# A streaming encoder trunk on one core: weights moved to multiples of 256 bytes, low parts first, the first norm one half product later, states in a pool of their own

## The chip, the core and the metric

The kernel runs on one core of one Trainium2 chip. The metric is the device time of one execution in microseconds, the median of three executions.

## What is computed

Two layers over 288 frames at once (256 of a new stream, 32 of a running one), width 2048, all in float32. Cut to what matters here:

```python
h = rmsnorm(x, g)                       # layer 0: retention and gated linear attention side by side
z = einsum('btd,de->bte', h, w_in)      # 2048 x 7184
o = concat(retention heads with state_ret, GLA heads with state_gla)   # 4 + 4 heads
x = x + einsum('bte,ed->btd', o, w_out)
g, u = split(rmsnorm(x) @ w_up)         # ConvFFN, D_FF = 5632
x = x + (silu(conv3(g)) * u) @ w_down
x = x + band_attention(rmsnorm(x) @ w_qkv) @ w_out_att    # layer 1: 16 heads
x = x + ConvFFN(rmsnorm(x)); y = rmsnorm(x)
```

Returned are y, the new retention and GLA states, the new keys and values and the last rows of each ConvFFN.

## The kernel before, in words

Features lie on the 128 partitions, the 288 frames (`T`) along the free axis. Every weight matrix is cut into tiles of 128 x 128; one product (128 outputs for all frames) sums over 16 tiles of its input (22 in the down projections), which arrive 8 at a time (`WCH`) as one DMA of 512 KB on SP's queue.

To keep float32 precision with the fast float32r matmul, each operand is split into a high part (rounded to float32r) and a low part (the rest). `weights` (L55) does this for a chunk of 8 weight tiles: `w` comes in, ScalarE casts it to `wh` (L62), VectorE subtracts to get `wl` (L63). The inputs `xx` (16 tiles of 2 x 288 numbers) and `bb` hold both parts of an input side by side, high first: bytes 0 to 1151 high, 1152 to 2303 low. For each weight tile TensorE then does three matmuls into one PSUM accumulator, which I call a triple:

- L91: `wh` times the first 320 columns (`TX`) of the pair, from byte 0: all 288 high ones, 32 low ones;
- L92: `wh` times the other 256 columns, from byte 1280, added to columns 32 to 287;
- L95: `wl` times the 288 high columns, from byte 0.

`joined` (L97) adds the 32 columns that went behind. In the built program every tile of `xx` and `bb` starts at a multiple of 256 bytes of its partition. The tiles `wh` and `wl` (three buffers each, 4096 bytes) start at 64 bytes past a multiple of 256, since the constants ahead of them end there; one weight tile of 128 columns is 512 bytes, so each of them starts 64 past a multiple. The exception is `lo_h`, the weights of the 16 gate columns in `first_products`, at 192 past one.

Tile, the layer the kernel is written in, sets the order on each engine from the order of the code and its own costs; each engine runs its queue in order. `run` (L210) opens the stages one after another, each with a pool of SBUF of its own: `in` (`start`, L262), `ab` (`ab_mixer`, layer 0's heads), then `x` with `f0`, `c` and `f1` in it. A pool's memory is given to the next one.

Around the places that change:

- `start` loads inputs and first weights in 12 pieces (`first_products`, L104), then does one value product `v0`, then the sum of squares on ScalarE and VectorE (`first_squares`, L144 to L155), then `norm_stat` (L202; its matmul is L207, then `rsqrt`, L164 to L174, which gives `R`), then the first half (`second(0)`, 8 triples) of the product `v1`. Its second half is `first[4](1)` in `gla_head` (L562), the first gate's matmul (L513) needs `R`.
- Each GLA head loads its state (`gst`, L567, 128 KB) and each retention head its own (`rst`, L738, 256 KB) into the pool `ab`, by DMA issued from GpSimd (POOL). The retention states are updated in place and written out by L832.
- `out_proj` (L289) for layer 0 loads `x` again by DMA from POOL (L294, 288 KB each). L304 adds a finished product to `x`; ScalarE and VectorE then prepare the next norm (L184 to L200).

Of the kernel before, what the change touches and what calls it, by code (L numbers as in the profile page):

```python
# [5 lines left out]
F32 = mybir.dt.float32  # L6
# [6 lines left out]
P = 128  # L13
D = 2048
KD = D // P
TP = 256
TS = 32
T = TP + TS
# [8 lines left out]
RANK = 16  # L27
# [5 lines left out]
GRP = P // TS  # L33
# [5 lines left out]
class Trunk:  # L39
# [52 lines left out]
        nc.tensor.matmul(ps[:, TX - T : T], lhsT=w, rhs=x[:, TX:], start=False, stop=last, skip_group_check=True)  # L92

    def high(self, ps, w, x, last):
        self.nc.tensor.matmul(ps[:, :T], lhsT=w, rhs=x[:, :T], start=False, stop=last, skip_group_check=True)  # L95

    def joined(self, ps):  # L97
        n = TX - T
# [111 lines left out]
    def run(self, ctx):  # L210
        nc, a = self.nc, self.a

        ones = self.const("ones", [P, P + 32])
        self.ones, self.eps = ones[:, :P], ones[:, P : P + 1]
        self.xx = [self.const(f"x{k}", [P, 2 * T], F32R) for k in range(KD)]
        self.xh, self.xl = [[x[:, c] for x in self.xx] for c in (slice(0, T), slice(T, 2 * T))]
        b_all = self.const("b", [P, KD, 2 * T], F32R)
        self.bh_all, self.bl_all = b_all[:, :, :T], b_all[:, :, T:]
        self.bb, self.bh, self.bl = [[x[:, k, :] for k in range(KD)] for x in (b_all, self.bh_all, self.bl_all)]
        self.R = self.const("R", [P, T])  # L220
        nc.vector.memset(self.ones, 1.0)
        nc.vector.memset(self.eps, EPS)
        self.gains = self.const("gains", [P, 5, KD], F32, a["gains"], nc.scalar)
        self.sq_last = None
        with self.tc.tile_pool(name="in", bufs=1) as pool:
            sums = self.start(pool)
        with self.tc.tile_pool(name="ab", bufs=1) as pool:
            self.ab_mixer(pool, *sums)
        with self.tc.tile_pool(name="x", bufs=1) as xp:

            x = xp.tile([P, KD * T + 16], F32, name="x", tag="x")[:, : KD * T].rearrange("p (k t) -> p k t", t=T)
            self.x = [x[:, k, :] for k in range(KD)]
            self.out_proj(a["w_out_ab"], 1, (WCH, 0), x)
            with self.tc.tile_pool(name="f0", bufs=2) as pool:
                self.ffn(pool, 0, 2, x)
            with self.tc.tile_pool(name="c", bufs=2) as pool:
                self.chain(
                    self.att_heads(pool), 3,
                    lambda: self.out_start(a["w_out_att"], (0, WCH), 2),
                )  # L240
            self.out_proj(a["w_out_att"], 3, (0, WCH))
            with self.tc.tile_pool(name="f1", bufs=2) as pool:
                self.ffn(pool, 1, 4, x)
# [18 lines left out]
    def start(self, pool):  # L262

        nc, a = self.nc, self.a
        w = a["w_in"]

        nc.scalar.activation(self.R[:, :1], self.ones[:, :1], AF.Abs_reciprocal_sqrt)
        xw = self._one(pool, "xw", [P, KD, T + N_FIRST * P + RANK])
        x_in = xw[:, :, :T]
        self.x = [x_in[:, k, :] for k in range(KD)]  # L270


        lo_h = self._one(pool, "lo_h", [P, KD, P], None, F32R)
        nc.gpsimd.memset(lo_h.bitcast(F32)[:, :, 2 * RANK :], 0.0)
        k0, q0, lo_ps = self.first_products(a["x_first"], xw, lo_h)
        self.ident = self.const("ident", [P, P], F32, a["ident"], nc.sync)

        self.w2 = self.const("w2", [P, 512 + 224])[: 2 * RANK + 1, :512]
        nc.sync.dma_start(self.w2, a["w2"])
        v0 = self.input_product(w[VB])  # L280
        self.first_squares(x_in)

        self.norm_stat()
        v1 = self.mm()
        second = lambda part: self.project(w[VB + 1], self.xx, KD, chunks=(0, WCH), part=part, ps=v1)
        second(0)
        return k0, q0, v0, lo_ps, second

    def out_proj(self, w, n, chunks, load=None):  # L289
# [23 lines left out]
    def ffn(self, pool, layer, n, x_all):  # L313
        nc, a = self.nc, self.a
        bb = self.bb + [self._one(pool, f"b{k}", [P, 2 * T], None, F32R) for k in range(KD, HALF)]
# [7 lines left out]
        last = layer == 1  # L323
        for half in range(2):
            for fl in range(HALF):
                f = half * HALF + fl
                g = self.input_product(up[f])
                u = self.input_product(up[NF + f])
                gp = gps[f % 3]
                nc.gpsimd.tensor_copy(gp[:, TP + 2 : TP + 4], hist[:, f, :])  # L330
                nc.vector.tensor_tensor(gp[:, 2 : TP + 2], g[:, :TP], self.R[:, :TP], op=ALU.mult)  # L331
                nc.vector.tensor_tensor(gp[:, TP + 4 :], g[:, TP:], self.R[:, TP:], op=ALU.mult)
                nc.gpsimd.tensor_copy(conv_out[:, f, 0:2], gp[:, TP : TP + 2])  # L333
                nc.gpsimd.tensor_copy(conv_out[:, f, 2:4], gp[:, T + 2 : T + 4])
                cw = convp[:, f, :]
                W = T + 2
                gc = pool.tile([P, W], F32, name="gc", tag="gc")
                nc.vector.tensor_scalar(gc, gp[:, 0:W], cw[:, 0:1], cw[:, 3:4], op0=ALU.mult, op1=ALU.add)
                for w in (1, 2):
                    nc.vector.scalar_tensor_tensor(  # L340
                        gc, gp[:, w : w + W], cw[:, w : w + 1], gc, op0=ALU.mult, op1=ALU.add
                    )
                s = pool.tile([P, W], F32, name="sg", tag="sg")
                nc.scalar.activation(s, gc, AF.Silu)
                v = pool.tile([P, T], F32, name="v", tag="v")
                nc.vector.tensor_tensor(v, u, self.R, op=ALU.mult)  # L346
                nc.vector.tensor_tensor(v[:, :TP], v[:, :TP], s[:, :TP], op=ALU.mult)
                nc.vector.tensor_tensor(v[:, TP:], v[:, TP:], s[:, TP + 2 :], op=ALU.mult)  # L348
                self.split(bb[fl][:, :T], bb[fl][:, T:], v)
            if last and half == 1:  # L350
                nc.scalar.activation(self.R[:, :1], self.ones[:, :1], AF.Abs_reciprocal_sqrt)
            if half == 1:
                nc.gpsimd.dma_start(a["conv_out"][:, layer], conv_out)
            for m in range(KD):
                ps = self.project(down[m], bb, HALF, half * HALF)
                nc.vector.tensor_tensor(self.x[m], self.x[m], ps, op=ALU.add)
                if half == 1:
                    if last:
                        self.square_in(m, m == KD - 1)
                        nc.scalar.activation(self.x[m], self.x[m], AF.Copy, scale=self.gains[:, n, m : m + 1])  # L360
                    else:
                        self.norm_in(m, n)
# [188 lines left out]
    def gla_head(self, pool, hd, w, sums, masks, eyem, hg, s4, sts, first):  # L551
        nc, a = self.nc, self.a
        k = first[0] if first else self.input_product(w[KB + hd])
        k = self.parted(pool, k, "k0", s4["k"][:, 0, hd, :])
# [3 lines left out]
        v = first[2] if first else self.input_product(w[VB + 2 * hd])  # L558
        v = [self.parted(pool, v, "v0", s4["v"][:, 0, hd, :])]
# [3 lines left out]
        v.append(self.parted(pool, v1, "v1", s4["v"][:, 1, hd, :]))  # L563
        gate = lambda i: self.gate(pool, w[GB + 2 * hd + i], i, s4["z"][:, i, hd, :])
        z = [gate(0)] if first else []
        st = pool.tile([P, 256], F32, name="gst", tag="gst", bufs=GRP)
        nc.gpsimd.dma_start(st, a["state_gla"][hd])  # L567
        sts.append(st)

# [14 lines left out]
        vt = self.to_tokens(pool, v, "vt", 256, bufs=2)  # L586
# [6 lines left out]
        for i, l in enumerate(LEVELS):  # L593
            qk = pool.tile([P, TP], F32, name="qk", tag="qk", bufs=3)
            self.decayed(qk, k, q, E[:, i, :], l)
            for t in range(2):
                x = qk[:, t * P : (t + 1) * P]
                rhs = _halves(x, l)[:, :, 1, :]
# [7 lines left out]
        ps = self.mm()[:, : 3 * P]  # L606
        nc.tensor.matmul(ps[:, :P], lhsT=qk[:, :P], rhs=qk[:, P:], start=True, stop=True)
        for t in range(2):
            c = slice(t * P, (t + 1) * P)
# [123 lines left out]
    def ret_head(self, pool, hd, w, cosR, sinR, kdec, hg, s4, sts, aside):  # L733
        nc, a = self.nc, self.a
        dec = pool.tile([P, 384], F32, name="dec", tag="dec")
        nc.gpsimd.dma_start(dec, a["dec"][hd])
        st = pool.tile([P, 2, 256], F32, name="rst", tag="rst", bufs=GRP)
        nc.gpsimd.dma_start(st, a["state_ret"][hd])  # L738
        sts.append(st.rearrange("p j v -> p (j v)"))

        def rope(base, name):
            z = [self.input_product(w[base + 2 * hd + i]) for i in range(2)]
# [9 lines left out]
        k = rope(KA, "k")  # L752
# [167 lines left out]
    def att_sample(self, pool, g, kept, v4, bd):  # L920
# [10 lines left out]
            nc.tensor.matmul(ps[c], lhsT=q[:, TP:], rhs=k[:, TP:], start=True, stop=True)  # L931
        pv = self.mm()[:, :P]
        nc.tensor.transpose(pv, v4[0].rearrange("p h t -> p (h t)"), self.ident)
        vt = pool.tile([P, P], F32, name="avt4", tag="avt4")
        nc.scalar.copy(vt, pv)
        s = pool.tile([P, T], F32, name="as4", tag="as4")
        own = pool.tile([P, GRP, TS], F32, name="own4", tag="own4")
        mx = pool.tile([P, 1], F32, name="mx4", tag="mx4")
        sm = pool.tile([P, 1], F32, name="sm4", tag="sm4")
        nc.vector.tensor_tensor(s, ps, bias, op=ALU.add)  # L940
        nc.vector.tensor_reduce(mx, s, axis=mybir.AxisListType.X, op=ALU.max, negate=True)
        nc.scalar.activation(s, s, AF.Exp, bias=mx, accum_out=sm)
# [18 lines left out]
        for i in range(2):  # L961
            for c, (_, _, vc) in zip(quarter, kept):
                nc.tensor.matmul(
                    po[c], lhsT=pT[:, 1 + i, c], rhs=vc[:, i, :], start=False, stop=i == 1, skip_group_check=True
                )
        o = pool.tile([P, P], F32, name="ao4", tag="ao4")
        nc.vector.tensor_scalar(o, po, sm, None, op0=ALU.mult)
        yield
        ps = self.mm()[:, :P]
# [139 lines left out]
```

## Time and profile before

| | |
|---|---|
| median of 3 runs | 2658.73 us (2657.0 to 2659.18) |
| the profiled execution's own time | 2656.71 us |
| its span, first to last instruction | 2654.9 us |
| mean granted TensorE clock | 0.997 |
| busy: TensorE, VectorE, ScalarE, GpSimd | 99%, 64%, 42%, 9% |
| read from and written to HBM | 434.69 MB and 10.40 MB, 168 GB/s over the span |

Every number below that is a duration or a start comes from this one profiled execution. In rows of the timeline the first column is the start in us from the span's start, the second the duration. Matmuls overlap in their pipeline: what a matmul costs is the step from its start to the next one's, not its duration. In rows of the windows view the columns are the window, its length, the busy time and count of each engine, the granted clock of TensorE, and the DMA engines' share and GB/s.

### The profile page before, as it was taken

To read this page: it belongs to the slowest core of one execution; us is meant where nothing else is said; L and a number is where in the kernel's file an instruction comes from. 1 tells how busy PE (TensorE), PEld (TensorE's weight loads), DVE (VectorE), ACT (ScalarE), POOL (GpSimd) and SP (SyncE) were. 2 spreads that over 40 slices of the span, in tenths; PEclk is the share of its full clock that TensorE was granted. 3 is DMA by queue.
4 is the path that set the end of the run, shared out by engine and by line. 5 is a ranking of instruction groups with operands and counts; after the bars stand their busy time and mean duration, and the time that the engine had idled before them with its cause. 6 is when DMAs were issued, how large, how long until landed. Compare 5 with 4: busy or idle time off the path is not lost.

```text
span 2654.9 us, 49383 instructions
## 1 busy us (share of the span) xinstructions
PE 2636.5 (99%) x20079; PEld 2618.0 (99%) x20079; DVE 1708.6 (64%) x3355; ACT 1123.6 (42%) x1511; POOL 228.9 (9%) x471
## 2 busy tenths in 40 slices
PE   9999999999999999999999999999999999999998
PEld 9999999999999999999999999999999999999997
DVE  8776666677775467776555555567777645777654
ACT  6554444443333333334444344444333333333443
POOL 3000001011110001110021110100111000111000
PEclk9999999999999999999999999999999999999999
DMA  6444555555555555555675565555555555555554
GB/s 231 152 132 160 161 162 168 184 166 167 168 167 162 169 171 168 167 170 163 169 213 181 177 188 167 160 168 165 169 167 170 161 168 173 167 167 168 166 169 132
DMA packets 127584, 448.31 MB, mean 169 GB/s; under 512 B 16155, under 2 KB 16475, under 8 KB 127356
## 3 DMA queue, kind: packets, MB, share of 16 engines
q1 hardware_dynamic: 119564, 424.47, 52.0%
q0 software_dynamic: 7648, 20.65, 2.5%
q8 instruction: 157, 2.57, 0.4%
q14 instruction: 71, 0.58, 0.1%
q10 hardware_dynamic: 144, 0.04, 0.0%
HBM read 434.69 MB, written 10.40 MB: 168 GB/s over the span
## 4 chain that ended last, share of the span: by engine, by line
PE 87%; issue 11%; DMA 0%; DVE 0%; POOL 0%; ACT 0%; DVEq 0%; POOLq 0%; ACTq 0%
PE acc L91 32%; PE acc L95 28%; PE acc L92 25%; PE mm L599 0%; PE mm L913 0%; PE mm L877 0%; DMA x<-in_xT 0%; DMA out_ret_out<-rst 0%; DVE y L370 0%; PE mm L876 0%; PE mm L207 0%; PE mm L914 0%; DMA gains<-in_gains 0%; PE mm L91 0%; PE mm L513 0%
## 5 line engine op out<-in xcount | busy, mean ns | idle before, releaser
L91 PE MATMUL acc<-x,wh 128*128 128x320 f32 x4464 | 1394.9, 313 | 0.3 <-DVE x L185 0.3
L62 ACT CAST wh<-w 128x1024 fp32r<-128x1024 f32 (+1 forms) x812 | 838.8, 1033 | 1288.1 <-PE acc L92 1044.7
L63 DVE TENSOR_TENSOR wl<-w,wh 128x1024 fp32r<-128x1024 f32 (+1 forms) x812 | 977.5, 1204 | 532.8 <-ACT wh L62 521.1
L95 PE MATMUL acc<-x,wl 128*128 128x288 f32 x4464 | 1298.4, 291 | 0.0
L92 PE MATMUL acc<-x,wh 128*128 128x256 f32 x4464 | 1246.5, 279 | 0.0
L91 PEld LDWEIGHTS acc<-x,wh 128*128 128x128 f32 x4464 | 838.4, 188 | 2.3 <-issue 1.1
L92 PEld LDWEIGHTS acc<-x,wh 128*128 128x128 f32 x4464 | 838.5, 188 | 0.8 <-issue 0.3
L95 PEld LDWEIGHTS acc<-x,wl 128*128 128x128 f32 x4464 | 836.9, 188 | 0.1
L91 PE MATMUL acc<-b,wh 128*128 128x320 f32 x1920 | 599.0, 312 | 1.9 <-ACT wh L62 1.9
L95 PE MATMUL acc<-b,wl 128*128 128x288 f32 x1920 | 560.3, 292 | 0.5 <-DVE wl L63 0.5
L92 PE MATMUL acc<-b,wh 128*128 128x256 f32 x1920 | 536.6, 280 | 0.0
L91 PEld LDWEIGHTS acc<-b,wh 128*128 128x128 f32 x1920 | 361.6, 188 | 2.7 <-ACT wh L62 2.4
L95 PEld LDWEIGHTS acc<-b,wl 128*128 128x128 f32 x1920 | 361.4, 188 | 1.1 <-DVE wl L63 0.8
L92 PEld LDWEIGHTS acc<-b,wh 128*128 128x128 f32 x1920 | 361.6, 188 | 0.0
L100 DVE COPY tail<-acc 128x32 f32<-128x32 f32 x376 | 72.0, 192 | 285.7 <-PE acc L95 282.9
L333 POOL COPY conv_out<-gp 128x2 f32<-128x2 f32 x88 | 100.3, 1140 | 1272.5 <-DVE gp L331 1272.5
L161 ACT CAST b<-v 128x288 fp32r<-128x288 f32 x88 | 38.1, 433 | 149.8 <-DVE v L348 149.8
L340 DVE SCALAR_TENSOR_TENSOR gc<-gp,convp,gc 128x290 f32<-128x290 f32 x176 | 91.8, 522 | 6.2
L101 DVE TENSOR_TENSOR acc<-acc,tail 128x32 f32<-128x32 f32 x376 | 74.8, 199 | 12.1
L162 DVE TENSOR_TENSOR b<-v,b 128x288 fp32r<-128x288 f32 x88 | 40.5, 460 | 44.0 <-ACT b L161 44.0
L331 DVE TENSOR_TENSOR gp<-acc,R 128x256 f32<-128x256 f32 x88 | 37.4, 425 | 9.1 <-DVE acc L101 0.5
L346 DVE TENSOR_TENSOR v<-acc,R 128x288 f32<-128x288 f32 x88 | 40.2, 457 | 3.0
(300 smaller groups left out, 1177.9 us busy)
## 6 DMA issues: line engine op xcount, KB each, us to landing
w<-in_w_ffn_up SPq DMA_DIRECT2D x352, 512.0 KB, 3.8
w<-in_w_ffn_down SPq DMA_DIRECT2D x128, 512.0 KB, 3.7
w<-in_w_in SPq DMA_DIRECT2D x108, 512.0 KB, 3.8
w<-in_w_qkv SPq DMA_DIRECT2D x96, 512.0 KB, 3.9
w<-in_w_ffn_down SPq DMA_DIRECT2D x64, 384.0 KB, 3.2
w<-in_w_out_ab SPq DMA_DIRECT2D x32, 512.0 KB, 3.8
w<-in_w_out_att SPq DMA_DIRECT2D x32, 512.0 KB, 3.7
x<-in_xT POOLq DMA_DIRECT2D x8, 288.0 KB, 5.0
```

The costliest lines, as they stand in the source:

```text
L62: nc.scalar.copy(h, w)
L63: nc.vector.tensor_tensor(l, w, h.bitcast(F32), op=ALU.subtract)
L91: nc.tensor.matmul(ps[:, :TX], lhsT=w, rhs=x[:, :TX], start=first, stop=last, skip_group_check=True)
L92: nc.tensor.matmul(ps[:, TX - T : T], lhsT=w, rhs=x[:, TX:], start=False, stop=last, skip_group_check=True)
L95: self.nc.tensor.matmul(ps[:, :T], lhsT=w, rhs=x[:, :T], start=False, stop=last, skip_group_check=True)
L100: self.nc.vector.tensor_copy(x, ps[:, T:TX])
L101: self.nc.vector.tensor_tensor(ps[:, :n], ps[:, :n], x, op=ALU.add)
L161: self.nc.scalar.copy(h, v)
L162: self.nc.vector.tensor_tensor(l, v, h.bitcast(F32), op=ALU.subtract)
L333: nc.gpsimd.tensor_copy(conv_out[:, f, 0:2], gp[:, TP : TP + 2])
L340: nc.vector.scalar_tensor_tensor(gc, gp[:, w : w + W], cw[:, w : w + 1], gc, op0=ALU.mult, op1=ALU.add)
L346: nc.vector.tensor_tensor(v, u, self.R, op=ALU.mult)
```

## The change

Three things change, and one makes room.

**Addresses.** The constant `w2` is padded by 208 numbers and not 224, so that everything behind it moves down by 64 bytes: `wh` and `wl` now start at multiples of 256. In each pair of `xx` and `bb` the low part stands first. L91 thus reads 288 low and 32 high columns from byte 0, L92 256 high columns from byte 1280, and `high` (L95) reads the high part from byte 1152, that is 128 past a multiple of 256 (before: byte 0). The column counts stay 320, 256, 288. `x` is padded by 32 so that the extra tiles of `bb` stay at multiples of 256. The tiles of the pool `ab` shift (most from 0 to 192 past a multiple).

**First norm.** `norm_stat` stands behind `second(0)` and not ahead of it.

**States.** All states have a pool `states` with four buffers of 2 KB, opened ahead of all stages and kept to the end: two GLA states share a buffer, each retention state has one, the third and fourth take the buffers that the GLA states leave. 8 KB more are taken to the end; in return `avt4`, `own4`, `mx4`, `sm4` and `ao4` of `att_sample` have one buffer and not two.

```diff
     def high(self, ps, w, x, last):
-        self.nc.tensor.matmul(ps[:, :T], lhsT=w, rhs=x[:, :T], start=False, stop=last, skip_group_check=True)
+        self.nc.tensor.matmul(ps[:, :T], lhsT=w, rhs=x[:, T:], start=False, stop=last, skip_group_check=True)
...
-        self.xh, self.xl = [[x[:, c] for x in self.xx] for c in (slice(0, T), slice(T, 2 * T))]
+        self.xl, self.xh = [[x[:, c] for x in self.xx] for c in (slice(0, T), slice(T, 2 * T))]
...
-        self.bh_all, self.bl_all = b_all[:, :, :T], b_all[:, :, T:]
+        self.bl_all, self.bh_all = b_all[:, :, :T], b_all[:, :, T:]
...
+        self.stp = ctx.enter_context(self.tc.tile_pool(name="states", bufs=GRP))
...
-            x = xp.tile([P, KD * T + 16], F32, name="x", tag="x")[:, : KD * T].rearrange("p (k t) -> p k t", t=T)
+            x = xp.tile([P, KD * T + 32], F32, name="x", tag="x")[:, : KD * T].rearrange("p (k t) -> p k t", t=T)
...
-        self.w2 = self.const("w2", [P, 512 + 224])[: 2 * RANK + 1, :512]
+        self.w2 = self.const("w2", [P, 512 + 208])[: 2 * RANK + 1, :512]
...
-        self.norm_stat()
         v1 = self.mm()
         second = lambda part: self.project(w[VB + 1], self.xx, KD, chunks=(0, WCH), part=part, ps=v1)
         second(0)
+        self.norm_stat()
...
-                self.split(bb[fl][:, :T], bb[fl][:, T:], v)
+                self.split(bb[fl][:, T:], bb[fl][:, :T], v)
...
-        st = pool.tile([P, 256], F32, name="gst", tag="gst", bufs=GRP)
-        nc.gpsimd.dma_start(st, a["state_gla"][hd])
-        sts.append(st)
+        if hd % 2 == 0:
+            st = self.stp.tile([P, 512], F32, name="st", tag="st")
+            sts += [st[:, :256], st[:, 256:]]
+        nc.gpsimd.dma_start(sts[hd], a["state_gla"][hd])
...
-        st = pool.tile([P, 2, 256], F32, name="rst", tag="rst", bufs=GRP)
-        nc.gpsimd.dma_start(st, a["state_ret"][hd])
-        sts.append(st.rearrange("p j v -> p (j v)"))
+        st = self.stp.tile([P, 512], F32, name="st", tag="st")
+        nc.gpsimd.dma_start(st.rearrange("p (j v) -> p j v", j=2), a["state_ret"][hd])
+        sts.append(st)
...
-        own = pool.tile([P, GRP, TS], F32, name="own4", tag="own4")
+        own = pool.tile([P, GRP, TS], F32, name="own4", tag="own4", bufs=1)
```

The order on the engines, at three places. TensorE at the first norm, the piece of the difference around L207 (`x_71` is the first of the 16 input tiles, `x_79` the ninth; `mm` is the accumulator of `v1`):

```order
-L207 MATMUL mm<-xw,ones 128x288
 L91 MATMUL mm<-x_71,wh 128x320
 L92 MATMUL mm<-x_71,wh 128x256
...
 L92 MATMUL mm<-x_78,wh 128x256
 L95 MATMUL mm<-x_78,wl 128x288
+L207 MATMUL mm<-xw,ones 128x288
 L91 MATMUL mm<-x_79,wh 128x320
```

The norm's matmul moves behind 8 triples. The gate's matmul, L513 before and L515 now, stood 2 triples into the second half of `v1`; it now stands right behind that half.

VectorE at the same place, now (L63 makes a `wl`, L154 is the last addition of the squares, L171 to L174 make `R`):

```order
L154 TENSOR_TENSOR xw<-xw 128x288
L63 TENSOR_TENSOR wl<-w,wh 128x1024
L507 MEMSET lo 33x288
L63 TENSOR_TENSOR wl<-w,wh 128x1024
L171 TENSOR_SCALAR rv<-mm 128x288
L173 TENSOR_TENSOR rs<-rs,rv 128x288
L174 SCALAR_TENSOR_TENSOR R<-rs,ry 128x288
```

One more L63, that of the first gate product's second chunk, now stands ahead of the norm; on ScalarE its cast (L62) likewise stands ahead of L170. Before, both stood behind.

POOL at the start, now (L131 and L132 split `lo_h`, L571 and L741 are the loads of the states):

```order
L276 MEMSET lo_h 128x16x96
L571 DMA st<-in_state_gla 128x256 x3
L131 CAST lo_h<-xw 128x16
L571 DMA st<-in_state_gla 128x256
L132 ISA
L132 TENSOR_TENSOR lo_h<-xw,lo_h 128x16
L131 CAST lo_h<-xw 128x16 x7
L131 CAST lo_h<-xw 128x2x16
L132 TENSOR_TENSOR lo_h<-xw,lo_h 128x16 x7
L741 DMA st<-in_state_ret 128x512
```

Before, no state was loaded until `lo_h` was done. Now the four GLA states and two retention states are issued among the first products. The other two retention loads come behind the output of the GLA states, whose buffers they take. At the end of `ab` POOL's order is as before: four DMAs of L832 (now L835), then two of L294 (now L296).

More of the change, by code (lines that the diff above doesn't have):

```diff
@@ L933, in att_sample @@
         nc.tensor.transpose(pv, v4[0].rearrange("p h t -> p (h t)"), self.ident)
-        vt = pool.tile([P, P], F32, name="avt4", tag="avt4")
+        vt = pool.tile([P, P], F32, name="avt4", tag="avt4", bufs=1)
         nc.scalar.copy(vt, pv)
         s = pool.tile([P, T], F32, name="as4", tag="as4")
-        own = pool.tile([P, GRP, TS], F32, name="own4", tag="own4")
-        mx = pool.tile([P, 1], F32, name="mx4", tag="mx4")
-        sm = pool.tile([P, 1], F32, name="sm4", tag="sm4")
+        own = pool.tile([P, GRP, TS], F32, name="own4", tag="own4", bufs=1)
+        mx = pool.tile([P, 1], F32, name="mx4", tag="mx4", bufs=1)
+        sm = pool.tile([P, 1], F32, name="sm4", tag="sm4", bufs=1)
         nc.vector.tensor_tensor(s, ps, bias, op=ALU.add)
@@ L965, in att_sample @@
                 )
-        o = pool.tile([P, P], F32, name="ao4", tag="ao4")
+        o = pool.tile([P, P], F32, name="ao4", tag="ao4", bufs=1)
         nc.vector.tensor_scalar(o, po, sm, None, op0=ALU.mult)
```

## The prediction

> **What bounds the kernel now.** I read the page first, then the windows, the timeline of TensorE and the waits. From the page, busy time by engine, the granted clock in 40 slices, and the groups that carry TensorE:
>
> ```profile
> PE 2636.5 (99%) x20079; PEld 2618.0 (99%) x20079; DVE 1708.6 (64%) x3355; ACT 1123.6 (42%) x1511; POOL 228.9 (9%) x471
> PEclk9999999999999999999999999999999999999999
> L91 PE MATMUL acc<-x,wh 128*128 128x320 f32 x4464 | 1394.9, 313 | 0.3 <-DVE x L185 0.3
> L91 PE MATMUL acc<-b,wh 128*128 128x320 f32 x1920 | 599.0, 312 | 1.9 <-ACT wh L62 1.9
> ```
>
> TensorE is the bound from end to end, and its work is 4464 + 1920 = 6384 triples. So two things can shorten the run: fewer ns per triple, or the few places where it stands still. Four stretches in the windows view (the first inside a ConvFFN; the second at half clock; the third and fourth around the two stalls):
>
> ```profile
> 1000.00:1240.00 240.00, 240.00 (x1832) 240.00 (x1831) 167.95 (x321) 93.70 (x116) 28.04 (x52) 1.00 0.54 167
> 457.40:462.40 5.00, 5.00 (x22) 5.00 (x22) 4.31 (x10) 1.97 (x4) 1.00 (x2) 0.50 0.82 246
> 453.55:462.72 9.17, 6.77 (x29) 6.21 (x28) 7.96 (x18) 5.99 (x12) 2.51 (x7) 0.63 0.55 157
> 28.34:38.62 10.28, 8.37 (x58) 7.51 (x57) 8.37 (x19) 6.63 (x10) 6.46 (x17) 1.00 0.76 237
> ```
>
> The first gives 240 us / 1832 = 131 ns a matmul, 393 ns a triple. One triple on the timeline at full clock, and one at half clock:
>
> ```profile
> 1900.06 0.31 PE L91 MATMUL acc<-x,wh 128*128 128x320 f32 x1
> 1900.21 0.28 PE L92 MATMUL acc<-x,wh 128*128 128x256 f32 x1
> 1900.32 0.29 PE L95 MATMUL acc<-x,wl 128*128 128x288 f32 x1
> 1900.45 0.31 PE L91 MATMUL acc<-x,wh 128*128 128x320 f32 x1
> ```
>
> ```profile
> 458.13 0.47 PE L91 MATMUL acc<-b,wh 128*128 128x320 f32 x1
> 458.40 0.41 PE L92 MATMUL acc<-b,wh 128*128 128x256 f32 x1
> 458.61 0.44 PE L95 MATMUL acc<-b,wl 128*128 128x288 f32 x1
> 458.85 0.47 PE L91 MATMUL acc<-b,wh 128*128 128x320 f32 x1
> ```
>
> At half clock the steps are 0.27, 0.21 and 0.24 us: 0.72 us for 864 columns, 1.2 columns a ns, and each step is exactly its columns by that rate. Twice that rate would be 360 ns a triple; the trace has 393. So at full clock 33 ns of each triple, 211 us of the run, go to something that the array's own clock doesn't explain and that vanishes when it asks for operands half as fast. Reading operands is the candidate, and that is what the addresses touch.
>
> **The change, part by part: addresses.** No instruction is added; 6384 triples read from other places. In the trace no weight tile starts at a multiple of 256, so the price must be bounded. The nearest rows are those of `lo_h`, whose weights lie at 192 and not at 64. One round of the first products, 8 matmuls:
>
> ```profile
> 14.86 0.30 PE L91 MATMUL acc<-x,wh 128*128 128x320 f32 x1
> ...
> 15.65 0.30 PE L91 MATMUL acc<-x,lo_h 128*128 128x320 f32 x1
> 15.79 0.28 PE L92 MATMUL acc<-x,lo_h 128*128 128x256 f32 x1
> 15.91 0.30 PE L91 MATMUL acc<-x,wh 128*128 128x320 f32 x1
> ```
>
> From 14.86 to 15.91 are 1.05 us for 2304 columns, 0.456 ns a column; the triple has 393 / 864 = 0.455. Going from 64 to 192 changes nothing. That is the end at zero. But a tile of 512 bytes at 64 or at 192 touches three blocks of 256 bytes in both cases; at a multiple it touches two. If the 33 ns are paid by the blocks that a triple touches, 9 for the loads now and 5 + 4 + 5 for the streams, then 6 in place of 9 loads leave 20 of 23 (the last stream, from 128 past a multiple, still touches 5), and the gain is 33 x 3 / 23 = 4.3 ns. If they are all paid by the loads, a third goes: 11 ns. So the gain lies between 0 and 11 ns; a loss isn't excluded (a rival below). I take the middle between the measured zero and the block count, 2.15 ns a triple, x 6384 = 13.7 us, since the measured rows can't tell the two apart and weigh as much as a count.
>
> **The states' own pool.** The second stall, at the end of layer 0's heads, in POOL's, ScalarE's and TensorE's timelines:
>
> ```profile
> 439.95 2.34 POOL L832 DMA_DIRECT2D out_ret_out<-rst  x4 [11.70 <-DVE rst L831]
> 446.79 1.08 POOL L294 DMA_DIRECT2D x<-in_xT  x2 [4.51 <-DMA out_ret_out<-rst]
> 453.13 0.54 ACT L184 ACTIVATE x<-x,gains 128x288 fp32r<-128x288 f32 x1 [7.76 <-DMA x<-in_xT]
> 454.66 1.03 ACT L62 CAST wh<-w 128x1024 fp32r<-128x1024 f32 x1
> 453.56 0.29 PE L95 MATMUL acc<-b,wl 128*128 128x288 f32 x1
> 455.75 0.55 PE L91 MATMUL acc<-b,wh 128*128 128x320 f32 x1 [1.90 <-ACT wh L62]
> 457.00 0.61 PE L95 MATMUL acc<-b,wl 128*128 128x288 f32 x1 [0.50 <-DVE wl L63]
> ```
>
> The load of `x` waits until the states are written out, since both used the memory of `ab`. VectorE and ScalarE stand behind that load with the next weights, TensorE runs dry at 453.69 and then runs at half clock until 462.7. Of the 29 matmuls of that window two started ahead of it and one at its end: 26 x 0.131 = 3.4 us of work in 9.15 us, 5.75 us lost. Now the states aren't part of `ab`, and L296 can follow the four output DMAs at 442.3, 4.5 us earlier. With them beside it on the DMA engines I let 1 us of that go. The weights were 2.1 us late, and `wl` another 0.8 us; 3.5 us cover both, just. Next late would be `wl`, by tenths. I take 5.7 us, bounds 2 (no clock recovered) and 5.75.
>
> **The first norm.** The first stall (TensorE, VectorE and ScalarE):
>
> ```profile
> 28.34 0.29 PE L95 MATMUL acc<-x,wl 128*128 128x288 f32 x1
> 30.54 0.72 PE L207 MATMUL mm<-xw,ones 128*128 128x288 f32 x2 [1.91 <-issue]
> 35.22 0.48 PE L513 MATMUL mm<-lo,w 33*128 33x288 f32 x1
> 29.98 0.46 DVE L154 TENSOR_TENSOR xw<-xw 128x288 f32<-128x288 f32 x1
> 27.97 1.22 DVE L63 TENSOR_TENSOR wl<-w,wh 128x1024 fp32r<-128x1024 f32 x1
> 28.55 1.04 ACT L62 CAST wh<-w 128x1024 fp32r<-128x1024 f32 x1 [2.09 <-PE acc L92]
> ```
>
> TensorE stops for 2.20 - 0.13 = 2.07 us until the squares are summed, though the weights of both halves of `v1` are ready (their second `wl` is that L63; the cast at 28.55 is already the gate's). Now the 8 triples fill the gap: 28.47 + 8 x 0.393 = 31.6, then L207. What is next late is the gate's matmul: it came 4.7 us behind L207, and ScalarE now has one more cast of 1.04 us to do at 31.6, of which some 0.4 delay L170. That makes 36.7. TensorE has the second half until 31.6 + 0.7 + 3.1 = 35.4 and waits 1.3 us. So 0.8 us are left of 2.07. Against that stand the loads of the states, now among the first inputs:
>
> ```profile
> 33.82 0.54 POOL L567 DMA_DIRECT2D gst<-in_state_gla  x1
> 4.23 0.40 POOL L132 TENSOR_TENSOR lo_h<-xw,lo_h 128x16 fp32r<-128x16 f32 x1
> GB/s 0 25 239 393 325 365 397 381 435 403 417 408 421 402 362 381 389 401 418 291 25 0 258 254 20 168 332 53 233 242 147 332 115 242 324 259 265 242 147 156
> ```
>
> The last row is the DMA view of the first 40 us, a slice each: the engines are full at some 400 GB/s until 19 us. 512 KB of GLA states at that rate are 1.3 us, put ahead of inputs that TensorE uses almost as they land; the 512 KB of retention states come later, when inputs are ahead. Each issue also takes 0.54 us of POOL, one of them ahead of the first L132. Most of it hides, since inputs arrive faster than TensorE eats them; I take 0.4 us, bounds 0 and 1.3. Together the start gains 0.4 us, bounds -0.5 and 2.1. Single buffers for `own4` and the rest cost nothing: they are used again one group of four heads later.
>
> **Sum.** 13.7 + 5.7 + 0.4 = 19.8 us. Against the profiled execution's own 2656.7 us that is 2636.9; it ran 2.0 us below the median of the three runs, on which I forecast: 2658.7 - 19.8 = 2638.9 us.
>
> **Rivals.**
>
> *Addresses do nothing.* For it: the `lo_h` rows; all old and new starts are multiples of 64 bytes. Against it: the 33 ns need some cause in reading. Time: 2658.7 - 6.1 = 2652.6. The Trainium skill, on its page "SBUF — State Buffer" (A bandwidth-pool intuition that's wrong), gives TensorE a second, independent read port for weights, and on "TensorE: Matmul & The Clock Gate" (Back-to-back issue gap) a gap of N / 2.4 + 2.5 ns; by these no address matters and a triple takes 367.5 ns. The trace has 393, so something the two rules leave out is at work.
>
> *Slower: loads and streams meet.* Before, a load started 64 bytes off the stream that runs beside it; now the loads beside L91 and L92 start at the same place within 256 bytes as those streams, both at zero. If that start is where they block each other, and costs per triple what the block count would gain, 4.3 ns, then 2652.6 + 27.4 = 2680. It decides from 6.1 us / 6384 = 1.0 ns a triple on. For it: the loss is there only at full rate, as in a collision. Against it: the steps in the timeline don't vary with the place of a tile within larger blocks.
>
> *The stall stays.* The `x` load may still wait for something of `ab`, or lands late behind 1 MB of output; with addresses that do nothing that is 2658.
>
> *Collisions end altogether.* Then up to 33 ns a triple go: 2652.6 - 211 = 2442. Nothing in the rows shows it but the half clock.
>
> **How the numbers follow.** Forecast (0 to 11 ns gained, both stalls as above): 0.50. Addresses do nothing: 0.28. Slower: 0.13. Stall stays: 0.05. Collisions end: 0.04. The range reaches from the forecast with 11 ns, 2652.6 - 70 = 2582, up to 2664, the upper edge of no change; about 0.17 lies outside. A measurement of this kernel can tell about 0.2%, 5.3 us, from no change. Faster by more: 0.50 + 0.04 and half of 0.28 (its 6.1 us lie close to the edge, with bounds on both sides) = 0.68. Within: 0.14 + 0.05 = 0.19. Slower: 0.13.
>
> **What would show it.** Right: the count of matmuls in 240 us of a ConvFFN rises from 1832 to about 1842; no wait of TensorE at the second stall and full clock through it; L207 without a wait and 1.3 us of wait at L515. If that count stays at 1832, the address step is wrong; below it, the rival with collisions is right. If ScalarE still waits more than 5 us for `x`, the step on the states is wrong.

## The result, and the profile after

The kernel after the change takes 2691.01 us (median of 4, 2678.76 to 2691.76), the kernel before in the same session 2657.86 us. The ratio is 1.0116, with a 95% interval of 1.009 to 1.0141: slower by 33 us, outside the forecast range. The profiled execution took 2678.76 us (span 2677.0). (Of e3, e8 and e13 one execution each, which the medians count, took 1.6 to 3 times as long as its others; of e13 it was the profiled one, so that kernel has times here and no rows.)

From the page of the kernel after: busy time, granted clock, and the groups of L91 and L95.

```profile
PE 2657.4 (99%) x20079; PEld 2638.3 (99%) x20079; DVE 1709.3 (64%) x3355; ACT 1126.0 (42%) x1511; POOL 228.5 (9%) x471
PEclk9999999999999999999999999999999999999999
L91 PE MATMUL acc<-x,wh 128*128 128x320 f32 x4464 | 1386.1, 311 | 2.0 <-DVE x L185 2.0
L95 PE MATMUL acc<-x,wl 128*128 128x288 f32 x4464 | 1313.0, 295 | 1.2 <-DVE wl L63 1.2
```

TensorE is busy for 20.9 us more with the same 20079 matmuls. The mean duration of L91 even fell (313 to 311 ns) and that of L95 rose (291 to 295): durations overlap and don't give the cost, steps do. So I read the windows, two of them inside ConvFFNs and one behind the second stall:

```profile
1000.00:1240.00 240.00, 240.00 (x1833) 240.00 (x1832) 168.58 (x321) 93.44 (x115) 29.08 (x55) 1.00 0.52 167
1760.00:2000.00 240.00, 240.00 (x1800) 239.77 (x1799) 164.57 (x308) 101.18 (x126) 21.54 (x42) 1.00 0.50 165
456.50:462.00 5.50, 4.14 (x30) 3.68 (x29) 5.36 (x13) 4.30 (x8) 2.12 (x5) 1.00 0.54 153
```

The same stretch from 1760 us on, before:

```profile
1760.00:2000.00 240.00, 240.00 (x1830) 239.71 (x1829) 167.42 (x314) 101.66 (x128) 23.20 (x45) 1.00 0.54 167
```

Before, the two ConvFFN windows held 1832 and 1830 matmuls, 393 ns a triple. After, one ConvFFN still has 1833, and the other 1800: 720 us / 1800 = 400 ns. In both the clock is full. So a triple has more than one lasting rate. On TensorE's timeline the step from L91 to L91 at the second rate is 0.41 us in rounded starts:

```profile
1899.94 0.31 PE L91 MATMUL acc<-x,wh 128*128 128x320 f32 x1
1900.09 0.28 PE L92 MATMUL acc<-x,wh 128*128 128x256 f32 x1
1900.21 0.30 PE L95 MATMUL acc<-x,wl 128*128 128x288 f32 x1
1900.35 0.31 PE L91 MATMUL acc<-x,wh 128*128 128x320 f32 x1
```

Over the whole trace the steps from one triple's L91 to the next one's (those under 450 ns, so without pauses and half clock) average 393.39 ns before (6198 triples) and 397.02 after (6207). If all 6384 triples pay it, the difference is 23.2 us. That is more than the whole 22.05 us by which the two profiled executions differ.

The order edits did save a little. TensorE's waits, after:

```profile
6.56 0.43 PE L95 MATMUL acc<-x,wl 128*128 128x288 f32 x2
7.96 0.39 PE L91 MATMUL acc<-x,wh 128*128 128x320 f32 x1 [0.97 <-DVE x L185]
...
38.19 0.29 PE L95 MATMUL mm<-x,wl 128*128 128x288 f32 x1
39.58 0.48 PE L515 MATMUL mm<-lo,w 33*128 33x288 f32 x1 [1.10 <-issue]
...
46.83 0.28 PE L92 MATMUL acc<-x,wh 128*128 128x256 f32 x1
48.31 0.40 PE L95 MATMUL acc<-x,wl 128*128 128x288 f32 x1 [1.20 <-DVE wl L63]
...
456.78 0.29 PE L95 MATMUL acc<-b,wl 128*128 128x288 f32 x1
457.70 0.42 PE L91 MATMUL acc<-b,wh 128*128 128x320 f32 x1 [0.62 <-ACT wh L62]
457.95 0.28 PE L92 MATMUL acc<-b,wh 128*128 128x256 f32 x1
458.97 0.41 PE L95 MATMUL acc<-b,wl 128*128 128x288 f32 x1 [0.74 <-DVE wl L63]
```

A wait is the step less that of the matmul ahead of it. The start has 1.1 us at 6.7 us and two like it (0.4 and 0.6 us) until 11.4; then come 1.26 us at L515, 1.36 at the `wl` of 46.83, and 0.79 and 0.90 at the second stall: 6.4 us in all. Another 0.6 us goes in small pieces: six matmuls with `lo_h`, from 15.20 to 16.57 us, take 1.37 us where their usual steps make 0.79. Before it was 2.07 + 5.75 = 7.8 us. So some 0.8 us were saved, and 23.2 lost.

### The profile page after: what moved, and what is told of

The parts are those of the page before. It is cut to its first block, busy times and chain, and to the rows that moved or that the text cites. A ratio compares the mean times of both kernels' runs of the same rounds, so it can differ in the third digit from the quotient of the medians.

```text
span 2677.0 us, 49377 instructions
## 1 busy us (share of the span) xinstructions
PE 2657.4 (99%) x20079; PEld 2638.3 (99%) x20079; DVE 1709.3 (64%) x3355; ACT 1126.0 (42%) x1511; POOL 228.5 (9%) x471
## 4 chain that ended last, share of the span: by engine, by line
PE 98%; DVE 1%; DMA 0%; ACT 0%; issue 0%; POOL 0%; SPq 0%; DVEq 0%; ACTq 0%
PE acc L91 35%; PE acc L95 31%; PE acc L92 28%; PE mm L602 0%; DMA xw<-in_x_first 0%; PE mm L916 0%; PE mm L880 0%; DMA hist<-in_hist 0%; PE mm L420 0%; PE mm L789 0%; ACT wh L62 0%; PE mm L668 0%; DVE y L372 0%; PE mm L879 0%; PE mm L631 0%
## 5 line engine op out<-in xcount | busy, mean ns | idle before, releaser
L62 ACT CAST wh<-w 128x1024 fp32r<-128x1024 f32 (+1 forms) x812 | 839.6, 1034 | 1305.2 <-PE acc L92 1048.2
L91 PE MATMUL acc<-x,wh 128*128 128x320 f32 x4464 | 1386.1, 311 | 2.0 <-DVE x L185 2.0
L63 DVE TENSOR_TENSOR wl<-w,wh 128x1024 fp32r<-128x1024 f32 (+1 forms) x812 | 977.3, 1204 | 542.5 <-ACT wh L62 531.6
L95 PE MATMUL acc<-x,wl 128*128 128x288 f32 x4464 | 1313.0, 295 | 1.2 <-DVE wl L63 1.2
L92 PE MATMUL acc<-x,wh 128*128 128x256 f32 x4464 | 1257.5, 282 | 0.0
L91 PEld LDWEIGHTS acc<-x,wh 128*128 128x128 f32 x4464 | 848.7, 190 | 4.8 <-ACT wh L127 2.2
L95 PEld LDWEIGHTS acc<-x,wl 128*128 128x128 f32 x4464 | 847.3, 190 | 1.5 <-DVE wl L63 1.4
L92 PEld LDWEIGHTS acc<-x,wh 128*128 128x128 f32 x4464 | 838.9, 188 | 0.8 <-issue 0.3
L91 PE MATMUL acc<-b,wh 128*128 128x320 f32 x1920 | 593.8, 309 | 0.6 <-ACT wh L62 0.6
L95 PE MATMUL acc<-b,wl 128*128 128x288 f32 x1920 | 565.8, 295 | 0.7 <-DVE wl L63 0.7
L92 PE MATMUL acc<-b,wh 128*128 128x256 f32 x1920 | 540.5, 282 | 0.0
L91 PEld LDWEIGHTS acc<-b,wh 128*128 128x128 f32 x1920 | 364.8, 190 | 1.3 <-ACT wh L62 1.2
L95 PEld LDWEIGHTS acc<-b,wl 128*128 128x128 f32 x1920 | 364.8, 190 | 1.2 <-DVE wl L63 1.0
L92 PEld LDWEIGHTS acc<-b,wh 128*128 128x128 f32 x1920 | 360.7, 188 | 0.0
```

What stands on the lines that cost most here:

```text
L62: nc.scalar.copy(h, w)
L63: nc.vector.tensor_tensor(l, w, h.bitcast(F32), op=ALU.subtract)
L91: nc.tensor.matmul(ps[:, :TX], lhsT=w, rhs=x[:, :TX], start=first, stop=last, skip_group_check=True)
L95: self.nc.tensor.matmul(ps[:, :T], lhsT=w, rhs=x[:, T:], start=False, stop=last, skip_group_check=True)
```

## The experiments

**e1: the change once more**, without an edit, to see whether the slow stretches lie at the same places.

> The changed kernel once more, beside the others on one chip. In its profile a triple takes 393 ns in some stretches and 400 ns in others (1174 triples at 393 and 89 at 400 between 470 and 1200 us, 1931 at 400 between 1720 and 2500 us). If the rate is chosen anew after each pause, the time falls anywhere between about 2656 us (all at 393) and 2693 us (all at 400, 16 ns x 2200 more than the profiled run); if it hangs on the addresses alone, the same stretches are slow again and the time is 2679 us.

2690.9 us, ratio 1.0122 (1.0106 to 1.0137). Two windows of its trace:

```profile
1000.00:1240.00 240.00, 240.00 (x1802) 240.00 (x1801) 166.41 (x317) 92.86 (x113) 29.41 (x55) 1.00 0.52 165
1760.00:2000.00 240.00, 240.00 (x1809) 239.77 (x1809) 164.51 (x305) 101.69 (x128) 20.03 (x39) 1.00 0.52 165
```

The first ConvFFN, quick in the other execution (x1833), is slow here. The rate doesn't belong to a place in the program; in the timelines it changes after pauses or after other matmuls, those of the heads and the two L207 of a norm (at 541.4 us of the first execution from 396.7 to 393.3 ns, at 1831.8 of e1 from 400.0 to 396.7), and then lasts.

**e2 to e4: the two address edits taken apart.** All keep the moved norm and the states' pool; `x` is padded so that the extra tiles of `bb` stay where the streams are, here and below. e2: low part first, weights back at 64.

```diff
-x = xp.tile([P, KD * T + 32], ...
+x = xp.tile([P, KD * T + 16], ...
-self.w2 = self.const("w2", [P, 512 + 208])
+self.w2 = self.const("w2", [P, 512 + 224])
```

e3: weights at 0, high part first again (`split` at L351 likewise); e4 has both edits.

```diff
-    matmul(ps[:, :T], lhsT=w, rhs=x[:, T:], ...
+    matmul(ps[:, :T], lhsT=w, rhs=x[:, :T], ...
-self.xl, self.xh = ...
+self.xh, self.xl = ...
-self.bl_all, self.bh_all = ...
+self.bh_all, self.bl_all = ...
```

> The changed kernel with the weights back at 64 past a multiple of 256, low parts still first (L95's stream from 128). Theory A, that loads which start at the same place within 256 bytes as the stream beside them cost the time: no triple at 400 ns for long, about 2656 us. Theory B, that the start of L95's stream at 128 costs it: the 400 ns stay, 2679 to 2693 us.

> The changed kernel with the high parts first again (L95's stream from 0), weights still at multiples of 256. Theory A: all three loads now start with their streams, triples of 400 ns or more, 2680 us or slower. Theory B: 393 ns throughout, about 2656 us.

> Both address edits undone: only the norm's new place and the states' own pool are left. If the addresses made the run slower, triples of 393 ns and about 2656 us, 1 to 2 us under the kernel before: the profile after shows 4.0 and 2.1 us of the old stalls gone and 4.7 us of new ones. If it was the moved instructions, the 400 ns stay and the time is 2679 us or more.

e2: 2693.95 us, ratio 1.0156 (1.0131 to 1.0181). e3: 2690.4 us, 1.0126 (1.0109 to 1.0143). e4: 2654.82 us, 0.9995 (0.9985 to 1.0004). One window each, in that order:

```profile
1760.00:2000.00 240.00, 240.00 (x1790) 239.79 (x1789) 162.27 (x303) 101.74 (x127) 20.08 (x39) 1.00 0.51 164
```

```profile
1760.00:2000.00 240.00, 240.00 (x1799) 239.76 (x1799) 163.30 (x305) 101.73 (x127) 20.00 (x39) 1.00 0.51 165
```

```profile
1760.00:2000.00 240.00, 240.00 (x1829) 239.71 (x1828) 167.46 (x314) 100.63 (x125) 23.19 (x45) 1.00 0.52 167
```

Each address edit alone costs the whole (399.74 and 398.96 ns a triple; e4 has 393.40), and the two don't add up. e4, the rest of the change alone, can't be told from the kernel before.

**e5 to e9: place or distance?** All are e4 with other pads. e5 and e6 put the weights at 128 and 192; e7 puts all 64 higher; e8 puts `wl` alone at 0, in a pool of its own behind 192 bytes (its `w2` is padded by 160, which moves the rest by 256); e9 has the weights at 0 and the streams at 192.

```diff
 e5 -const("w2", [P, 512 + 224])  +const("w2", [P, 512 + 176])
 e6 -const("w2", [P, 512 + 224])  +const("w2", [P, 512 + 192])
 e7 -const("ones", [P, P + 32])   +const("ones", [P, P + 48])
    -const("w2", [P, 512 + 224])  +const("w2", [P, 512 + 160])
 e8 +self.pad = pool("pad", 1).tile([P, 48], F32, name="pad", tag="pad")
    +self.wlp = pool("wtl", 3)
    -l = self.wp.tile(...         +l = self.wlp.tile(...
 e9 -const("ones", [P, P + 32])   +const("ones", [P, P + 16])
```

> High part first, weights at 128 past a multiple of 256 (the two order edits stay). So far 64 with high first ran at 393 ns a triple, and 0 ran at 399. Theory R (what counts is where a load starts against the stream that runs beside it; a distance of 64 is quick, 0 is slow, and 192, the distance of the last stream in the low-first kernel with weights at 64, is slow too): 128 has not been seen; half a block away from the stream it should be no worse than 64, so 393 ns and 2655 us. Theory W (only weights that start at 64 are quick, by their own place): about 399 ns and 2690 us.

> High part first, weights at 192 past a multiple of 256. Theory R: the load starts 192 behind the stream, the distance that ran slowly with the low part first and weights at 64; 397 to 400 ns and 2685 to 2695 us. Theory W: the same, about 2690 us. A third possibility, that any weights which straddle blocks of 256 bytes are quick and only whole blocks are slow: 393 ns and 2655 us.

> High part first, streams at 64 and weights at 128 past a multiple of 256: everything 64 higher, the distance of 64 between load and stream kept. Theory R (the distance counts): 393 ns and 2655 us. Theory W, or any theory by which the absolute place of the weights or of the streams counts: slow, 397 to 400 ns and 2685 to 2695 us, unless weights at 128 with streams at 0 turn out quick as well.

> High part first, wh at 64 as before, wl alone at 0. One of the three loads of a triple then starts where its neighbouring stream starts, two do not. If each load pays for itself, a third of the 6 ns: 395 ns a triple and 2667 us. If a single load in the slow place is enough to lock the whole triple into the slow rhythm: 399 ns and 2690 us. If only the loads of wh count: 393 ns and 2655 us.

> High part first, weights at 0 as the change has them, and all streams at 192: a load again starts 64 past the stream beside it, which was quick with streams at 0 and at 64. Theory R (the distance between load and stream counts, not the place): 393 ns a triple and 2655 us. Theory W (weights that start at a multiple of 256 are slow by themselves): 399 ns and 2690 us.

| | weights | streams of L91, L92, L95 | ns a triple | median us | ratio, interval |
|---|---|---|---|---|---|
| e5 | 128 | 0, 0, 0 | 394.04 | 2659.35 | 1.0028 (1.0004 to 1.0052) |
| e6 | 192 | 0, 0, 0 | 393.97 | 2663.17 | 1.0023 (1.0014 to 1.0033) |
| e7 | 128 | 64, 64, 64 | 393.39 | 2655.4 | 0.9995 (0.9985 to 1.0004) |
| e8 | `wh` 64, `wl` 0 | 0, 0, 0 | 393.67 | 2656.79 | 1.0 (0.999 to 1.0009) |
| e9 | 0 | 192, 192, 192 | 393.41 | 2656.85 | 0.9998 (0.9989 to 1.0007) |

e9's weights stand at multiples of 256 as the change has them, and its window is that of the kernel before:

```profile
1760.00:2000.00 240.00, 240.00 (x1829) 239.71 (x1829) 167.46 (x314) 101.49 (x127) 23.19 (x45) 1.00 0.53 167
```

Theory W falls: the place of the weights costs nothing. With all streams at one place it is the distance from stream to load: 0 is slow, 64 is quick at all three places tried (streams at 0, 64 and 192), 128 and 192 are nearly as quick (three of e5's ten times lie between 2674 and 2686 us, so 128 slips into a slower rate now and then). My guess for e6, slow, was wrong. e8 also says that the load of `wl` at distance 0 is not enough by itself, nor pays a third; whether the loads of `wh` alone count, or it takes more than one load, stays open.

**e10 to e15 without e11 and e12: why the low part first is slow though its loads are off their streams.** e10 and e15 are the changed kernel with weights at 192 and 128 (`w2` padded by 192 and 176, `x` by 48 and 0). e13 is e4, and e14 is e2, each with one other start of L95:

```diff
 e13 -rhs=x[:, :T]  +rhs=x[:, TS : TS + T]
 e14 -rhs=x[:, T:]  +rhs=x[:, T - TS : 2 * T - TS]
```

> Low part first with weights at 192 (the streams of a triple start at 0, 0 and 128). With weights at 64 this order ran at 399.7 ns, at 0 at 398 to 400. If only a distance of 0 between a load and its stream were slow, 64 would have been quick, and 192 would be quick too: 393 ns and 2655 us. If the order of the parts is slow whatever the weights, since the third stream starts half a block off the other two: 398 to 400 ns and 2685 to 2695 us.

> High part first, weights at 64, both order edits in: the kernel that ran at 393.4 ns a triple. The one change: L95 reads its 288 columns from byte 128 of the pair and not from byte 0 (256 high columns and 32 low ones, so the products differ from the reference's). If the start of the third stream is what makes the low part first slow: 399 to 400 ns and 2690 us. If it is something else in that order: 393.4 ns and 2655 us.

> Low part first, weights at 64: the kernel that ran at 399.7 ns a triple. The one change: L95 reads its 288 columns from byte 1024 and not from byte 1152 (32 low columns and 256 high ones, so the products differ from the reference's). If the start of the third stream is the cause: 393.4 ns and 2655 us. If not: 399.7 ns and 2694 us.

> Low part first, weights at 128: the loads start 128 off the first two streams and at the same place as the third. If a load that starts where its stream starts is slow whichever it is: 399 ns and 2690 us. If the half block between the third stream and the other two is the only trouble: between 395.6 and 399.7 ns as with weights at 192 and 64, 2668 to 2694 us.

| | weights | streams of L91, L92, L95 | ns a triple | median us | ratio, interval |
|---|---|---|---|---|---|
| e10 | 192 | 0, 0, 128 | 395.55 | 2668.44 | 1.0038 (1.0025 to 1.0052) |
| e13 | 64 | 0, 0, 128 | | 2693.79 | 1.0124 (1.0103 to 1.0146) |
| e14 | 64 | 0, 0, 0 | 393.39 | 2655.12 | 0.9993 (0.9984 to 1.0002) |
| e15 | 128 | 0, 0, 128 | 396.62 | 2675.08 | 1.0065 (1.005 to 1.008) |

e14, then e15:

```profile
1760.00:2000.00 240.00, 240.00 (x1830) 239.71 (x1829) 167.50 (x315) 100.63 (x125) 23.10 (x45) 1.00 0.53 167
```

```profile
1760.00:2000.00 240.00, 240.00 (x1814) 239.74 (x1813) 164.85 (x308) 101.40 (x127) 21.63 (x42) 1.00 0.52 165
```

This settles which edit it is. e13 and e14 differ from their models in nothing but the start of L95's 288 columns: moving it to 128 makes the quick kernel slow by 1.2%, moving it to 0 makes the slow one quick. (Both multiply `wl` with some columns of the wrong part, so their products are not the kernel's; the counts of columns are the same.) With the third stream 128 bytes off the other two, all four places of the weights are slow, by 2 to 6 ns a triple. For e10 neither given answer came: 395.55 ns lies between 393 and 398, though none of its loads is at distance 0 from a stream (192 from the first two, 64 from the third). For e15 the first answer falls, since 396.62 is not 399 though a load starts where the third stream starts, and the second, 395.6 to 399.7, holds. What in the chip the three streams share, so that 128 bytes cost time, no run shows.

**e11 and e12: a version that beats both.** High part first, weights at 64; the states' loads held until `R` is there; the first two loads of `x` ahead of three of the four state outputs. e11 has the norm where the kernel before has it, e12 where the change puts it. In the edit below the copies from `R` are what holds the loads.

```diff
+nc.vector.tensor_copy(st[:, :512:256], self.R[:, :2])
 nc.gpsimd.dma_start(sts[hd], a["state_gla"][hd])
...
-nc.gpsimd.dma_start(a["ret_out"][h, :, 1], ...)
+self.late.append((a["ret_out"][h, :, 1], ...))
...
 piece(2, 2)
+for o, s in self.late:
+    nc.gpsimd.dma_start(o, s)
```

> Both address edits undone, the first norm back ahead of the half product, the states in their own pool, but their loads held until R is there (as late as before the change), and the first two loads of x ahead of three of the four last state outputs. Theory: the start is that of the kernel before (2.1 us at the norm, no waits for inputs), the wait of 1.7 us and the half clock at the end of layer 0's heads are gone. Against the kernel before 2.1 + 0.8 + 2.9 us less: 2651 us. Rival: x lands no earlier for going first, since the same bytes share the DMA engines; then 1.7 us stay and it is 2652.5 us.

> The same with the first norm behind the half product, as the change has it. Theory: the move takes 2.07 us away and brings 1.3 at the gate and 1.4 at the wl behind it, so 0.6 us more than with the norm ahead: 2651.5 us. Rival: the wait for wl came from the early state loads and goes with them; then 0.7 us less than with the norm ahead.

e11: 2652.58 us, ratio 0.998 (0.9971 to 0.9989). e12: 2652.07 us, 0.9979 (0.997 to 0.9988), 5.25 us under the kernel before (2657.32 beside them). POOL, ScalarE and TensorE in e12:

```profile
439.10 0.54 POOL L303 DMA_DIRECT2D out_ret_out<-st  x1 [11.83 <-DVE st L839]
439.92 1.07 POOL L297 DMA_DIRECT2D x<-in_xT  x2 [0.29 <-issue]
445.94 0.54 ACT L184 ACTIVATE x<-x,gains 128x288 fp32r<-128x288 f32 x1 [4.51 <-DMA out_ret_out<-st]
35.08 0.29 PE L95 MATMUL mm<-x,wl 128*128 128x288 f32 x1
36.51 0.48 PE L518 MATMUL mm<-lo,w 33*128 33x288 f32 x1 [1.13 <-issue]
```

With `x` first ScalarE uses it 6.8 us behind the first output (9.6 in the changed kernel), and TensorE has no wait there at all: so the rival, by which going first would not make `x` land earlier, falls. In e12 the wait at L515 (now L518) is TensorE's only one above 0.4 us between its first triple and the last norm, 1.3 us in place of 7.8; its profiled execution, the quickest of its ten, took 2650.36 us, 6.35 below that of the kernel before. e11 keeps the 2.07 us at the norm. Its median is the rival's 2652.5 and not the 2651 expected, but by another way: a `wl` comes 0.5 us late at 45.0 us, where I had expected no wait. The medians of e11 and e12 differ by 0.5 us, which these times can't tell from nothing.

## Why the prediction was wrong, step by step

**The address term** (13.7 us gained by forecast; 23 lost in the profiled execution, some 34 in the others). The step that failed is "the 33 ns are paid by the blocks that a triple touches". The count of blocks has no price: before, a triple touches 23; e3 touches 20 and is slower by 5.6 ns, e8 22 and e7 25 at 393.67 and 393.39 ns. Nor has the place of the weights by itself (e9). What has one is where two things that are read at the same time stand to each other: a load against its stream (e3: 398.96 - 393.39 = 5.6 ns a triple, lost), and the third stream against the first two (e13, e14). Both edits of the change move from the quick place to a slow one. I had bounded a gain by two rows and left the loss to a rival, though the same 33 ns allow both signs: they show a loss at full clock that is gone at half clock, not which way a move goes. The `lo_h` rows, taken as "the end at zero", compared distances of 64 and 192 from the stream, which e4 and e6 find nearly alike (393.40 and 393.97 ns); the change's own distance, 0, was not in any row, and that should have kept the loss as wide as the gain.

**The rival "loads and streams meet"** gave 2680 us at 4.3 ns and had 0.13. Its mechanism is shown for the loads (e3 against e4, e9 against e3), at 5.6 ns. It missed the third stream, and that edit alone is enough (e2, e13). The Trainium skill, on its page "SBUF — State Buffer" (A bandwidth-pool intuition that's wrong), gives weights a read port of their own; e3 and e4 differ in addresses alone, and 5.6 ns a triple lie between them, so the rule doesn't cover this case. The 367.5 ns that the prediction worked out beside it are no fair test of the other rule: the Trainium skill, on "TensorE: Matmul & The Clock Gate" (Back-to-back issue gap), gives N / 2.4 + 2.5 for a single matmul, and says that in a stream of loads and matmuls both set the spacing. The forecast's other rival, that addresses do nothing, falls with it.

**The states' pool** (5.7 us gained by forecast; 4.1 measured: 5.75 less the 0.79 and 0.90 that stay). The half clock went as forecast (1.00 in the window from 456.50). The failed step is "3.5 us cover both, just". POOL and ScalarE, after:

```profile
446.20 2.33 POOL L835 DMA_DIRECT2D out_ret_out<-st  x4 [11.82 <-DVE st L834]
448.74 1.07 POOL L296 DMA_DIRECT2D x<-in_xT  x2 [0.20 <-ACT wh L62]
455.84 0.54 ACT L184 ACTIVATE x<-x,gains 128x288 fp32r<-128x288 f32 x1 [7.28 <-DMA hist<-in_hist]
```

L296 does follow the four outputs, and the use of `x` did come 3.5 us earlier: 9.64 us behind the first output, 13.18 before. But the order moved too. VectorE before, then after, between the state update (438.97 and 445.23) and the first addition to `x`:

```profile
442.30 1.23 DVE L63 TENSOR_TENSOR wl<-w,wh 128x1024 fp32r<-128x1024 f32 x1 [0.51 <-ACT wh L62]
...
445.40 1.22 DVE L63 TENSOR_TENSOR wl<-w,wh 128x1024 fp32r<-128x1024 f32 x1 [0.53 <-ACT wh L62]
452.52 0.82 DVE L304 TENSOR_TENSOR x<-x,acc 128x288 f32<-128x288 f32 x2 [5.89 <-DMA hist<-in_hist]
```

```profile
448.59 1.23 DVE L63 TENSOR_TENSOR wl<-w,wh 128x1024 fp32r<-128x1024 f32 x1 [0.56 <-ACT wh L62]
455.23 0.45 DVE L306 TENSOR_TENSOR x<-x,acc 128x288 f32<-128x288 f32 x1 [5.41 <-DMA convp<-in_convp]
```

The addition now stands one L63 earlier in the queue; that Tile put it there because it expects `x` earlier is my reading, not shown. One chunk of weights, 8 triples or 3.1 us of TensorE's work, now waits behind `x` instead of lying ready, and eats nearly all of the 3.5 us: counted from the state update, TensorE now runs dry 3.0 us earlier than before. My test for this step, a ScalarE wait above 5 us, came out against it (7.28 us) and was a poor one: ScalarE waits longer when it has less to do ahead.

**The first norm** (0.4 us gained by forecast; some 3 lost). L207 has no wait and L515 has 1.26 us, as forecast (1.3). The term that was too small is that of the states' loads: they cost 2.1 us of waits for inputs and the 0.6 us at `lo_h`, above my bound of 1.3. POOL issued three of them at 2.05 us, beside the very first inputs. TensorE's 166th matmul starts at 24.93 us before and at 27.86 after; at the old addresses it starts at 26.66 with the loads early (e4) and at 24.88 with them held (e12). Whether POOL's time or the bytes did it was not tried apart. And a wait of 1.36 us came at 46.83, where I had said nothing. VectorE and POOL ahead of it:

```profile
42.74 0.29 DVE L644 TENSOR_TENSOR E<-sums 128x128 f32<-128x128 f32 x1
42.95 0.92 DVE L643 TENSOR_TENSOR E<-sums 128x128 f32<-128x128 f32 x1
43.79 0.28 DVE L644 TENSOR_TENSOR E<-sums 128x128 f32<-128x128 f32 x1
43.99 1.31 DVE L643 TENSOR_TENSOR E<-sums 128x128 f32<-128x128 f32 x1
...
47.04 2.35 DVE L63 TENSOR_TENSOR wl<-w,wh 128x1024 fp32r<-128x1024 f32 x2
42.82 0.90 POOL L536 TENSOR_TENSOR cosR<-cosR,R 128x288 f32<-128x288 f32 x1 [2.24 <-DMA cosR<-in_cos]
...
44.32 0.82 POOL L536 TENSOR_TENSOR sinR<-sinR,R 128x288 f32<-128x288 f32 x1
```

POOL's two multiplications by `R` fall on VectorE's chain for `E`; two L643 of 0.28 us take 0.92 and 1.31, and each ends about 0.15 us behind POOL's. That is 1.7 us on the chain that the next L63 waits for. Before, the same pair cost this chain 0.9 us (two steps of it, at 39.88 and 40.35 us, took 0.54 and 0.89 us) and TensorE did not wait. In e12 the E chain is done at 42.3 and the wait is gone; whether the held loads, the order or the collision did that was not tried apart. The Trainium skill, on "SBUF — State Buffer" (SBUF: two separate sides), has VectorE and GpSimd share a pair of ports that the one that starts first holds for a whole instruction. The first pair of rows agrees; in the second L643 starts ahead of POOL's row and still ends behind it, and spans on POOL are rough.

## What to carry to other kernels

Where TensorE is the bound, the addresses of what it reads at the same time, within 256 bytes, are worth 1.2 to 1.6% here, and "aligned" is not "quick": keep the starts of all streams alike and the weights off them (64 bytes here), and measure a shift of the whole layout by one pad before building on it. Count matmuls in a fixed window; durations hide such a loss, and the time of a whole execution mixes several rates. And when a load is made earlier, look at what the order puts behind it: a queue that expects it early will wait for it early.

## What the runs showed that I had not expected

- A triple at full clock keeps a rate for hundreds of microseconds and then takes another: 393 and 400 ns (x1833 and x1800 in 240 us of one execution). The quick steady rate is 393.33 ns over the 1852 triples of e4 between 470 and 1200 us, the slow one 400.0. Other rates last as well. Some are a short pattern that repeats: steps of 393 and 400 ns in turn, mean 396.66, in e1 from 1840 to 2640 us, and about 393, 394 and 399 in turn, mean 395.56, in e10 from 550 to 1370 us. The slowest is a mean of 402.22 in e2 from 1840 to 2640 us. With 2.4 columns a ns, twice the 1.2 of the half clock, 393.33 and 400.0 are 944 and 960 columns, 59 and 60 times 16 columns or 64 bytes; the patterns fit such units only over two or three triples. Why was not tried.
- GpSimd and VectorE can each hold the other up: in the rows above VectorE loses 0.64 and 1.03 us, and in e12 POOL's multiplication, 0.90 us above, lasts 5.40 us while VectorE is busy without a pause (spans on POOL are rough, and that the one causes the other is read from the times alone):

```profile
39.94 5.40 POOL L539 TENSOR_TENSOR cosR<-cosR,R 128x288 f32<-128x288 f32 x1 [2.25 <-DMA cosR<-in_cos]
```
